# Gate pairs of a decoder layer on one Trainium2 core: the norm's product one step later, the GELU gates one pair later, and three LRU steps from GpSimd to ScalarE and VectorE

## The chip, the core and the metric

The kernel runs on one core of a Trainium2 chip: one launch computes a whole decoder layer in float32. The time is that of the device in microseconds, lower is better; the median of three runs is the figure to forecast. Five engines work side by side: TensorE does matrix products, VectorE (DVE in the profile) elementwise work and scans, ScalarE (ACT) functions and copies, GpSimd (POOL) elementwise work and the issue of transfers, SyncE (SP) the issue of transfers alone. Each runs its own instructions strictly in order, and waits for another engine or a transfer by semaphores.

## The reference, cut to what matters

```python
h = h + W_out( sum_k sigmoid(g_k(xn)) * P_k(mixer_k(xn)) )      # xn = RMSNorm(h), 1024 tokens x 1024
h = h + W2 relu(W1 RMSNorm(h))^2
# mixer A (gMLP), mixer B (RG-LRU, 8 heads of 128), mixer C (SSD, 4 groups)

# B: the LRU
r = sigmoid(xh @ w_r + b_r);  i = sigmoid(xh @ w_i + b_i)
log_a = -8 * r * softplus(-lam);  a = exp(log_a)
inp = sqrt(-expm1(2 * log_a)) * (i * xb)
h_t = a_t * h_{t-1} + inp_t
y_b = gelu(gate) * h

# C: what follows the scan of SSD
y = y * silu(z)
y_c = norm_g * y * rsqrt(mean(y * y over its group of 256 channels) + EPS)
```

All gates (`g_k`, `gate`, `z`) are column blocks of one input product `xn @ w_in`.

## The kernel before

Every product is done in three passes on halves that are split into a high and a low part (`split`, L132 on ScalarE and L133 on VectorE: high·high, high·low, low·high). Channels lie on the 128 partitions, tokens along a row, so that one output block is 128 channels by 1024 tokens; half 0 and half 1 are its first and last 512 tokens.

**Order of the stages.** The first 130 us or so form the norm and its transposes. Until about 600 us "units" follow: `one_unit` multiplies 128 columns of `w_in` by `xn` (48 matmuls, L555), hands the result to a `post` function, and calls `step`, which advances every waiting generator by one piece. These generators are the stages of the SSD groups (`ssd_stages`, four groups) and of the LRU heads (`stages` inside `lru_units`, eight heads). This part is ordered by the framework's planner, which may exchange instructions of one engine. From about 640 to 1022 us the pair loop runs, in which the order is that of the code (`manual_schedule`). Then come the products of the three branches, `w_out`, and the MLP to the end.

**An LRU head**, for each half: three matmuls (L789) for each of the two gates, tanh (L792), exp and tanh (L796, L797), two combined steps on VectorE (L798, L799), `m + 1` on GpSimd (L800), a square root on ScalarE (L801), a combined step on VectorE (L802), a product on GpSimd (L803), and the scan on VectorE (L804). Heads 6 and 7 also multiply by their GELU gate on GpSimd (L807). The GpSimd queue also issues transfers, among them the reads of `acs_d` (L657) that the next SSD group needs and the write of its output (L732).

**A pair** is 256 columns of `w_in` by 1024 tokens. A scheme with seven products instead of eight block products computes it; each product is 12 matmuls of 128x512. Kinds of pair: "t" (a branch's gate: tanh, written to scratch), "z" (SSD's output times silu(z), the norm over the group, written to `yd["c"]`) and "g" (an LRU gate). In each turn of the loop the products are p1, p2, then p4 of the pair before, then p5, p6, p3, p7, and a `step` follows each: seven steps in a turn. The operands of the next pair are made in the same turn (`cast1`, `sums1`, `sums2`, `cast12`, `cast22`, `cast34`: L132 and L133, L502 to L507).

**The norm of a z pair** is the generator `post_z(half)`, one for each half. Half 1 starts at the last step of its own turn; half 0 is done by p4 in the next turn, and idles for three steps first. Its pieces, one a step: tanh and a combined step (L949, L950); the product with SSD's output and the square (L952, L953); the sum of two squares (L955); nothing; the matmul with `ones` that sums over the channels into `vs`, and a square root (L959, L961); the reciprocal (L963); two small steps that read `vs` (L965, L966); two more (L968, L969); the scaled result and its write (L973, L974). Before, half 1's product so stands behind p5 of the turn after the z pair, and half 0's behind p4 and ahead of p5 of the turn after that.

The list `pairs` gives the order of the pairs: before, t z t g t t z t g t t z t g t z t t t.

Of the kernel before, what the change touches and what calls it, by code (L numbers as in the profile page):

```python
# [11 lines left out]
AF = mybir.ActivationFunctionType  # L12
ALU = mybir.AluOpType
# [23 lines left out]
def trunk_kernel(ctx: ExitStack, tc: tile.TileContext, x, norm_mix_g, w_in, b_gate, gmlp_ln_g, gmlp_ln_b,  # L37
# [4 lines left out]
    nc = tc.nc  # L42
    x, w_in, b_gate, out = x[0], w_in[0], b_gate[0], out[0]
# [24 lines left out]
    def nm(s):  # L68
        uid[0] += 1
        return f"{s}_{uid[0]}"  # L70

    def act(shape=(P, T), dt=F32):
        return pools[0].tile(list(shape), dt, tag="act", name=nm("a"))

    def half_(shape=(P, HF), dt=F32):
        return halfp.tile(list(shape), dt, tag="half", name=nm("h"))

    def aux():
        return auxp.tile([P, HF], F32, tag="aux", name=nm("aux"))
# [6 lines left out]
    tt = nc.vector.tensor_tensor  # L86
    stt = nc.vector.scalar_tensor_tensor
    ts = nc.vector.tensor_scalar
    actv = nc.scalar.activation
    mm = nc.tensor.matmul  # L90

    def hsl(h):
        return slice(h * HF, h * HF + HF)
# [34 lines left out]
    def split(dst_hi, dst_lo, src, eng=None, cast=None):  # L128
        if cast:
            cast.tensor_copy(out=dst_hi, in_=src)  # L130
        else:
            actv(dst_hi, src, AF.Copy)  # L132
        (eng or nc.vector).tensor_tensor(out=dst_lo, in0=src, in1=dst_hi.bitcast(F32), op=ALU.subtract)  # L133
# [99 lines left out]
    def gelu2(dst, ps, w):  # L233
        sq = act()[:, :w]
        actv(sq, ps, AF.Square)
        stt(out=sq, in0=sq, scalar=1.0 / GELU_C, in1=ps, op0=ALU.add, op1=ALU.mult)
        actv(sq, sq, AF.Tanh, scale=GELU_S * GELU_C)
        stt(out=dst, in0=sq, scalar=1.0, in1=ps, op0=ALU.add, op1=ALU.mult)  # L238
# [212 lines left out]
    for q in range(2):  # L451
# [3 lines left out]
        for i in range(4):  # L455
            g = q * 4 + i
# [79 lines left out]
    def later(gen):  # L536
        pending.append(gen)
# [33 lines left out]
    def unit_in(col, post):  # L571
        unit(w_in[:, col:col + P], X, post)


    def conv(dst, ps, taps, bias):
        actv(dst, ps, AF.Identity, scale=taps[3], bias=bias)
        for j in (1, 2, 3):
            stt(out=dst[:, j:], in0=ps[:, :T - j], scalar=taps[3 - j], in1=dst[:, j:], op0=ALU.mult, op1=ALU.add)
# [173 lines left out]
    def lru_units(h):  # L752
        S = {}

        def post_x(ps):
            xb = S["xb"] = act()
            conv(xb, ps, [va[:, LCW + j * 8 + h:LCW + j * 8 + h + 1] for j in range(4)], va[:, LCB + h:LCB + h + 1])
            wraw = lrup.tile([P, 256], F32, tag="lr", name=nm("lr"))
            tc.keep_in_program_order(nc.sync.dma_start(out=wraw[:, :P], in_=lru_w_r[0, h]))
            tc.keep_in_program_order(nc.sync.dma_start(out=wraw[:, P:], in_=lru_w_i[0, h]))  # L760
            S["w"] = [lrup.tile([P, 256], F32R, tag=f"lw{i}", name=nm("lw")) for i in range(2)]
            split(S["w"][0], S["w"][1], wraw)
            S["xs"] = []
            for half in range(2):
                p_ = half_(dt=F32R), half_(dt=F32R)
                split(p_[0], p_[1], xb[:, hsl(half)])
                S["xs"].append(p_)
            if h < PLAIN:
                later(stages(False))
            elif h == 7:  # L770
                v_group(0)

        def post_g(ps):
            S["g2"] = act()
            gelu2(S["g2"], ps, T)
            later(stages(True))

        def stages(gated):
            if not gated:
                yield  # L780
            xb, w = S["xb"], S["w"]
            y = act()
            for half in range(2):
                tk = hsl(half)
                tri_ = []
                for q in range(2):
                    ps = aux()
                    for n, (wi, ai) in enumerate(((0, 0), (0, 1), (1, 0))):
                        mm(ps, w[wi][:, q * P:(q + 1) * P], S["xs"][half][ai], start=(n == 0), stop=(n == 2))  # L789
                    t = half_()  # L790
                    o = (LBR, LBI)[q] + h
                    actv(t, ps, AF.Tanh, scale=0.5, bias=vh[:, o:o + 1])  # L792
                    tri_.append(t)
                tr, ti = tri_
                m = half_()
                actv(m, tr, AF.Exp, scale=s2[:, h:h + 1], bias=s2[:, h:h + 1])  # L796
                actv(tr, tr, AF.Tanh, scale=s1[:, h:h + 1], bias=s1[:, h:h + 1])  # L797
                stt(out=m, in0=m, scalar=1.0, in1=tr, op0=ALU.add, op1=ALU.mult)  # L798
                stt(out=tr, in0=m, scalar=2.0, in1=m, op0=ALU.add, op1=ALU.mult)  # L799
                nc.gpsimd.tensor_scalar(out=m, in0=m, scalar1=1.0, scalar2=1.0, op0=ALU.mult, op1=ALU.add)  # L800
                actv(tr, tr, AF.Sqrt, scale=-1.0 / 16)  # L801
                stt(out=ti, in0=ti, scalar=1.0, in1=xb[:, tk], op0=ALU.add, op1=ALU.mult)  # L802
                nc.gpsimd.tensor_tensor(out=ti, in0=ti, in1=tr, op=ALU.mult)  # L803
                nc.vector.tensor_tensor_scan(out=y[:, tk], data0=m, data1=ti, initial=(0.0 if half == 0 else y[:, HF - 1:HF]),  # L804
                                             op0=ALU.mult, op1=ALU.add)
            if gated:
                nc.gpsimd.tensor_tensor(out=S["g2"], in0=y, in1=S["g2"], op=ALU.mult)  # L807
                nc.gpsimd.dma_start(out=yd["b"][h], in_=S["g2"])
            else:
                nc.gpsimd.dma_start(out=hr_d[h], in_=y)  # L810

        unit_in(C_XB + h * P, post_x)
        if h >= PLAIN:
            unit_in(C_GATE + h * P, post_g)
# [4 lines left out]
    def v_group(g):  # L819
        if g < 8:  # L820
            v_of[g] = act((P, NCH, P))
            nc.gpsimd.dma_start(out=v_of[g], in_=vn_d[:, g * P:(g + 1) * P].rearrange("(c p) d -> p c d", p=P))
# [75 lines left out]
    def actx():  # L898
        return actx_pool[0].tile(list(two), F32, tag="actx", name=nm("x"))

    class Pair:
# [42 lines left out]
        def post_z(self, half):  # L944
            o, y, t = self.o[half], self.y[half], actx()
            if half == 0:
                for _ in range(3):
                    yield
            actv(t, o, AF.Tanh, scale=0.5)  # L949
            stt(out=o, in0=t, scalar=1.0, in1=o, op0=ALU.add, op1=ALU.mult)  # L950
            yield
            tt(out=o, in0=o, in1=y, op=ALU.mult)  # L952
            actv(t, o, AF.Square)  # L953
            yield
            tt(out=t[:, 0], in0=t[:, 0], in1=t[:, 1], op=ALU.add)  # L955
            yield
            yield
            vs = aux()
            mm(vs, ones, t[:, 0], start=True, stop=True)  # L959
            r, q = y[:, 0], y[:, 1]  # L960
            actv(r, vs, AF.Sqrt, scale=1.0 / 256, bias=eps4)  # L961
            yield
            nc.vector.reciprocal(out=r, in_=r)  # L963
            yield
            tt(out=q, in0=r, in1=r, op=ALU.mult)  # L965
            stt(out=q, in0=vs, scalar=256 * 4.0 * EPS, in1=q, op0=ALU.add, op1=ALU.mult)  # L966
            yield
            ts(out=q, in0=q, scalar1=-0.5 / 256, scalar2=1.5, op0=ALU.mult, op1=ALU.add)  # L968
            tt(out=r, in0=r, in1=q, op=ALU.mult)  # L969
            yield  # L970
            for b in range(2):
                col = SNG + self.e + b
                stt(out=o[:, b], in0=o[:, b], scalar=va[:, col:col + 1], in1=r, op0=ALU.mult, op1=ALU.mult)  # L973
            nc.gpsimd.dma_start(out=self.part(yd["c"], half), in_=o)  # L974
# [41 lines left out]
    pairs = [(br, e) for br in (2, 1, 0) for e in range(0, KD, 2)]  # L1016
    pairs = [("t",) + p_ for p_ in pairs]
    for i in range(3):
        pairs.insert(5 * i + 1, ("z", 0, 2 * i))
        pairs.insert(5 * i + 3, ("g", 0, 2 * i))  # L1020
    pairs.insert(15, ("z", 0, 6))
    cur = []

# [609 lines left out]
    with tc.manual_schedule():  # L1633
# [159 lines left out]
        for n in range(NB):  # L1793
            j, i = divmod(n, 7)
# [58 lines left out]
```

## Time and profile before

| | |
|---|---|
| median of 3 runs | 2010.82 us (2010.63 to 2010.97) |
| profiled execution | 2009.9 us; its span 2007.9 us |
| TensorE busy | 1923.5 us, 96% |
| VectorE, ScalarE, GpSimd busy | 1406.7 (70%), 1005.3 (50%), 293.1 us (15%) |
| mean granted clock of TensorE | 0.982 of full speed |
| stage of the pairs | about 640 to 1022 us |
| stage of SSD and LRU units | about 130 to 600 us |

How to read it: TensorE is the engine that is nearly always busy, so time can be lost in two ways only: it stands idle, or its clock is lowered. In rows of the timeline the bracket at the end of a row gives the idle time before it and what ended that; in rows of the chain the first number is the start, the second the length. Rows of the windows give, for a stretch, the busy time and instruction count of TensorE's matmuls, its weight loads, VectorE, ScalarE and GpSimd, then the granted clock, the busy share of the transfer engines and GB/s.

### The profile page before, as it was taken

How to read it: one execution, taken by the hardware profiler on the slowest of the kernel's cores; microseconds unless marked ns; L12 is line 12 of the kernel's file. 1: busy time of each engine (PE TensorE's matmuls, PEld its weight loads, DVE VectorE, ACT ScalarE, POOL GpSimd, SP SyncE). 2: the span in 40 equal slices, each digit the busy share in tenths (PEclk: the TensorE clock that was granted, in tenths of full speed). 3: DMA queues.
4: the chain of work that ended last, by engine and by line, in shares of the span. 5: the costliest groups of instructions: out<-in, count | busy, mean ns of one | idle time of the engine just before them, and what ended most of it. 6: DMA issues, size and time to landing. Idle time of an engine off the chain costs nothing.

```text
span 2007.9 us, 23777 instructions
## 1 busy us (share of the span) xinstructions
PE 1923.5 (96%) x8928; PEld 1596.5 (80%) x8928; DVE 1406.7 (70%) x2000; ACT 1005.3 (50%) x1455; POOL 293.1 (15%) x392
## 2 busy tenths in 40 slices
PE   8999999999999999998999999998999999999996
PEld 7998878787787787787788888786788887888885
DVE  5485868686668766666758789436765557787787
ACT  6425858576533445444554544246555555253243
POOL 4112313233333000000010111000111110000000
PEclk9999999999999999999999999999999999999998
DMA  4246465465654242525289787521544448644532
GB/s 158 66 140 145 118 138 132 110 146 130 146 145 139 92 147 74 171 77 162 74 277 282 208 270 193 173 95 53 168 163 137 162 155 301 193 138 135 189 109 91
DMA packets 211015, 301.25 MB, mean 150 GB/s; under 512 B 13028, under 2 KB 125876, under 8 KB 210900
## 3 DMA queue, kind: packets, MB, share of 16 engines
q1 hardware_dynamic: 167348, 158.54, 26.2%
q0 software_dynamic: 34544, 119.69, 21.9%
q10 hardware_dynamic: 9008, 21.51, 3.0%
q8 instruction: 70, 1.15, 0.2%
q14 instruction: 45, 0.37, 0.1%
HBM read 195.75 MB, written 74.58 MB: 135 GB/s over the span
## 4 chain that ended last, share of the span: by engine, by line
PE 55%; DVE 11%; ACT 6%; issue 4%; DMA 2%; POOL 0%; ACTq 0%; SPq 0%; DVEq 0%; POOLq 0%
PE aux L478 39%; PE gps L478 8%; PE ps L555 4%; PE aux L1375 2%; DMA wt<-in_w_branch_c_dram 1%; ACT wt L132 1%; DVE wt L133 1%; DMA a<-acs_d 1%; DVE a L133 1%; ACT a L1424 1%; DVE rsq_q L111 1%; PE aux L959 1%; DVE b L133 1%; ACT a L132 1%; PE aux L836 0%
## 5 line engine op out<-in xcount | busy, mean ns | idle before, releaser
L555 PE MATMUL ps<-xn,wh 128*128 128x512 f32 x1088 | 295.6, 393 | 0.0
L478 PE MATMUL aux<-b,b 128*128 128x512 f32 x1152 | 264.3, 389 | 0.3 <-DVE b L133 0.2
L478 PEld LDWEIGHTS aux<-b,b 128*128 128x128 f32 x1152 | 215.9, 188 | 46.3 <-DVE b L133 1.6
L555 PEld LDWEIGHTS ps<-xn,wh 128*128 128x128 f32 x1088 | 203.7, 189 | 42.4 <-issue 0.3
L478 PE MATMUL aux<-a,b 128*128 128x512 f32 x960 | 219.4, 389 | 0.0
L478 PEld LDWEIGHTS aux<-a,b 128*128 128x128 f32 x960 | 180.2, 188 | 37.4
L555 PE MATMUL ps<-xn,wl 128*128 128x512 f32 x544 | 167.6, 389 | 0.0
L478 PE MATMUL gps<-xn,wt 128*128 128x512 f32 x684 | 160.2, 392 | 2.1 <-DVE a L238 2.1
L478 PE MATMUL aux<-b,wt 128*128 128x512 f32 x672 | 156.9, 389 | 0.0
L478 PEld LDWEIGHTS gps<-xn,wt 128*128 128x128 f32 x684 | 129.4, 189 | 29.4 <-issue 2.5
L478 PEld LDWEIGHTS aux<-b,wt 128*128 128x128 f32 x672 | 126.2, 188 | 26.2
L133 DVE TENSOR_TENSOR wt<-a,wt 128x1024 fp32r<-128x1024 f32 x66 | 80.9, 1225 | 89.0 <-ACT wt L132 88.9
L132 ACT ACTIVATE b<-wt 128x1024 fp32r<-128x1024 f32 x88 | 90.7, 1053 | 87.3 <-DMA wt<-u_d 62.5
L555 PEld LDWEIGHTS ps<-xn,wl 128*128 128x128 f32 x544 | 102.2, 188 | 21.6
L133 DVE TENSOR_TENSOR b<-wt,b 128x1024 fp32r<-128x1024 f32 x88 | 107.2, 1219 | 17.3 <-ACT b L132 17.2
L1605 DVE TENSOR_TENSOR a<-aux,a 128x512 f32<-128x512 f32 x112 | 77.0, 688 | 50.0 <-PE aux L478 50.0
L133 DVE TENSOR_TENSOR a<-a,a 128x1024 fp32r<-128x1024 f32 (+1 forms) x68 | 66.6, 985 | 41.5 <-ACT a L132 41.5
L133 DVE TENSOR_TENSOR wt<-rt,wt 128x1024 fp32r<-128x1024 f32 x35 | 42.8, 1224 | 66.8 <-ACT wt L132 66.8
L478 PE MATMUL aux<-a,wt 128*128 128x512 f32 x336 | 78.7, 390 | 3.3 <-ACT a L1482 3.3
L132 ACT ACTIVATE a<-a 128x1024 fp32r<-128x1024 f32 (+1 forms) x68 | 55.8, 837 | 50.3 <-DVE a L1557 45.4
L478 PEld LDWEIGHTS aux<-a,wt 128*128 128x128 f32 x336 | 62.9, 188 | 17.2 <-ACT a L1482 4.2
L132 ACT ACTIVATE wt<-a 128x1024 fp32r<-128x1024 f32 x66 | 69.6, 1054 | 7.0 <-DVE a L506 6.7
(350 smaller groups left out, 3570.5 us busy)
## 6 DMA issues: line engine op xcount, KB each, us to landing
wt<-u_d SPq DMA_DIRECT2D x54, 512.0 KB
u_d<-a POOLq DMA_DIRECT2D x48, 512.0 KB, 5.6
raw<-in_w_in_dram SPq DMA_DIRECT2D x34, 512.0 KB
wl<-raw POOLq DMA_DIRECT2D x34, 512.0 KB, 5.2
g_d<-a POOLq DMA_DIRECT2D x24, 512.0 KB, 3.4
a<-g_d ACTq DMA_DIRECT2D x24, 512.0 KB
rt<-in_w_in_dram SPq DMA_DIRECT2D x19, 512.0 KB
a<-in_w_in_dram SPq DMA_DIRECT2D x19, 512.0 KB
```

What stands on the lines that cost most here:

```text
L111: stt(out=q, in0=r, scalar=nh, in1=r, op0=ALU.mult, op1=ALU.mult)
L132: actv(dst_hi, src, AF.Copy)
L133: (eng or nc.vector).tensor_tensor(out=dst_lo, in0=src, in1=dst_hi.bitcast(F32), op=ALU.subtract)
L478: mm(ps, lhs[l][kk], rhs[r][kk], start=(new and n == 0), stop=(n == 11), skip_group_check=not new)
L555: mm(ps[:, hsl(h)], w[wi][:, k, :], a.rhs(ai, k, h), start=(n == 0), stop=(n == 3 * KD - 1))
L959: mm(vs, ones, t[:, 0], start=True, stop=True)
L1375: mm(ps, M.tok(a, k, c), wo[nb][k][w], start=(k == 0 and a + w == 0), stop=(k == KD - 1 and a == 1))
L1424: actv(Nf[th, k // 2][:, k % 2, (c % 4) * P:(c % 4 + 1) * P], ps[:, i * P:(i + 1) * P], AF.Identity, scale=g2c[:, KD + k:KD + k + 1])
L1605: tt(out=h, in0=ps, in1=h, op=ALU.add)
```

## The change

Three edits:

1. `post_z` gets one more empty step between the sum L955 and the norm's matmul. The matmul, and every later piece of the generator with it, stands one step (one product) later.
2. Each of the three "g" pairs stands one place later in the list. The order becomes t z t t g t z t t g t z t t g z t t t.
3. In the LRU stages `m + 1` becomes a ScalarE activation, and the products L803 and, for the two gated heads, L807 become VectorE tensor-tensor instructions.

```diff
@@ LRU stages
-                nc.gpsimd.tensor_scalar(out=m, in0=m, scalar1=1.0, scalar2=1.0, op0=ALU.mult, op1=ALU.add)
+                actv(m, m, AF.Identity, bias=1.0)
                 actv(tr, tr, AF.Sqrt, scale=-1.0 / 16)
                 stt(out=ti, in0=ti, scalar=1.0, in1=xb[:, tk], op0=ALU.add, op1=ALU.mult)
-                nc.gpsimd.tensor_tensor(out=ti, in0=ti, in1=tr, op=ALU.mult)
+                tt(out=ti, in0=ti, in1=tr, op=ALU.mult)
...
             if gated:
-                nc.gpsimd.tensor_tensor(out=S["g2"], in0=y, in1=S["g2"], op=ALU.mult)
+                tt(out=S["g2"], in0=y, in1=S["g2"], op=ALU.mult)
@@ post_z
             tt(out=t[:, 0], in0=t[:, 0], in1=t[:, 1], op=ALU.add)
             yield
             yield
+            yield
             vs = aux()
@@ pairs
         pairs.insert(5 * i + 1, ("z", 0, 2 * i))
-        pairs.insert(5 * i + 3, ("g", 0, 2 * i))
+        pairs.insert(5 * i + 4, ("g", 0, 2 * i))
```

From L955 on, line numbers after the change are one higher (L959 becomes L960). Where the instructions now stand, at three places:

TensorE, two turns after the first z pair, before. `gps_5718` is what p4 adds to, `aux_5917` is p5's result, `ones` the norm's operand of half 0:

```order
L478 MATMUL gps_5718<-a_5433,a_5693 128x512
L478 MATMUL gps_5718<-a_5432,a_5693 128x512
L959 MATMUL aux_5914<-x_5771,ones 128x512
L478 MATMUL aux_5917<-h_5061,wt_5810 128x512
L478 MATMUL aux_5917<-h_5062,wt_5810 128x512
```

The same place after the change, where `aux_5914` is p5's result and `gps_5857` is what p6 adds to:

```order
L478 MATMUL gps_5718<-a_5432,a_5693 128x512
L478 MATMUL aux_5914<-h_5061,wt_5807 128x512
...
L478 MATMUL aux_5914<-h_5401,wt_5808 128x512
L960 MATMUL aux_5934<-x_5771,ones 128x512
L478 MATMUL gps_5857<-h_4972,wt_5807 128x512
```

All 12 matmuls of p5 now stand between p4 and the norm's matmul of half 0, which is the first row ahead of p6.

VectorE, the rows that lead to half 0's sum (L955), before. `x_5655` belongs to half 1, `a_5602` and `x_5771` to half 0; `wt_5875` is an operand of the next turn:

```order
L963 RECIPROCAL x_5655<-x_5655 128x512
L1001 TENSOR_TENSOR a_5785<-aux_5772,a_5785 128x512
L133 TENSOR_TENSOR a_5828<-a_5715,a_5828 128x512
L965 TENSOR_TENSOR x_5655<-x_5655 128x512
L966 SCALAR_TENSOR_TENSOR x_5655<-aux_5792,x_5655 128x512
L950 SCALAR_TENSOR_TENSOR a_5602<-x_5771,a_5602 128x1024
...
L952 TENSOR_TENSOR a_5602<-a_5602,x_5709 128x1024
L133 TENSOR_TENSOR wt_5875<-a_5789,wt_5874 128x1024
L973 SCALAR_TENSOR_TENSOR a_5653<-a_5653,va,x_5655 128x512 x2
L955 TENSOR_TENSOR x_5771<-x_5771 128x512
```

And after, the names as before but for the operand, which is `wt_5873`:

```order
L1002 TENSOR_TENSOR a_5785<-aux_5772,a_5785 128x512
L133 TENSOR_TENSOR a_5827<-a_5715,a_5827 128x512
L964 RECIPROCAL x_5655<-x_5655 128x512
L950 SCALAR_TENSOR_TENSOR a_5602<-x_5771,a_5602 128x1024
...
L952 TENSOR_TENSOR a_5602<-a_5602,x_5709 128x1024
L133 TENSOR_TENSOR wt_5873<-a_5789,wt_5872 128x1024
L969 TENSOR_SCALAR x_5655<-x_5655 128x512
L970 TENSOR_TENSOR x_5655<-x_5655 128x512
L955 TENSOR_TENSOR x_5771<-x_5771 128x512
L986 TENSOR_TENSOR a_5870<-gps_5879,a_5870 128x512
L974 SCALAR_TENSOR_TENSOR a_5653<-a_5653,va,x_5655 128x512 x2
```

Half 1's reciprocal moved behind two rows of the pair, half 1's L969 and L970 moved to just ahead of half 0's sum, and the two scaling rows (before L973, now L974) moved from ahead of that sum to behind it.

GpSimd, where the last SSD group begins beside LRU head 6, before. `h_` tiles and `a_4335` are the LRU's, `a_4528` and `a_4531` the rows of `acs_d` that the SSD group needs, `a_4490` is the gMLP's input:

```order
L800 TENSOR_SCALAR h_4380<-h_4380 128x512
L800 TENSOR_SCALAR h_4402<-h_4402 128x512
L803 TENSOR_TENSOR h_4378<-h_4378,h_4372 128x512
L803 TENSOR_TENSOR h_4400<-h_4400,h_4394 128x512
L822 DMA a_4490<-vn_d 128x8x128
L807 TENSOR_TENSOR a_4335<-a_4367,a_4335 128x1024
L657 DMA a_4528<-acs_d 128x512
L808 DMA yb_d<-a_4335 128x1024
```

And after:

```order
L528 DMA wl_4417<-raw_4414 128x1024
L822 DMA a_4490<-vn_d 128x8x128
L657 DMA a_4528<-acs_d 128x512 x2
L657 DMA a_4531<-acs_d 128x512
L808 DMA yb_d<-a_4335 128x1024
```

The five computing rows are gone from the queue, and three reads of `acs_d` stand ahead of the write of the LRU's output. In three SSD groups the planner also changed ScalarE's order around the first step of a convolution (L576), which before stood behind a split of the LRU's weights (L132 `lw`) that waits for a transfer:

```order
L527 ACTIVATE wl_4040<-wh_4039 128x1024
L632 ACTIVATE a_4015<-a_4010 128x1024
L132 ACTIVATE lw_4208<-lr_4205 128x256
L526 ACTIVATE wh_4146<-raw_4144 128x1024
L576 ACTIVATE a_4093<-ps_4044,vh,scw 128x1024
```

and after stands ahead of it:

```order
L527 ACTIVATE wl_4040<-wh_4039 128x1024
L632 ACTIVATE a_4015<-a_4010 128x1024
L576 ACTIVATE a_4093<-ps_4044,vh,scw 128x1024
L526 ACTIVATE wh_4146<-raw_4144 128x1024
L132 ACTIVATE lw_4208<-lr_4205 128x256
```

The split with its wait moved behind the convolution's first step. ScalarE has 45 loads of a function table before and after.

## The prediction

> **What bounds the kernel now.** I read the page first, then TensorE's table of waits, then its timeline at the longest of them, the chain of waits there, and the clock by windows.
>
> ```profile
> span 2007.9 us, 23777 instructions
> PE 1923.5 (96%) x8928; PEld 1596.5 (80%) x8928; DVE 1406.7 (70%) x2000; ACT 1005.3 (50%) x1455; POOL 293.1 (15%) x392
> ```
>
> TensorE is the bound: it rests 84 of 2007.9 us. The change takes no matmul away, so it can gain only idle time and lowered clock. Who makes TensorE wait (total, times, longest):
>
> ```profile
> PE aux L959 <- DVE x L955: 19.3, 4, 4.8
> PE aux L789 <- ACT a L677: 4.2, 1, 4.2
> PE aux L789 <- DVE h L714: 3.3, 2, 2.0
> PE aux L478 <- ACT a L991: 3.0, 3, 1.0
> PE aux L703 <- DVE h L673: 2.1, 2, 1.2
> PE aux L703 <- ACT a L576: 2.1, 1, 2.1
> PE aux L789 <- DVE h L729: 1.9, 3, 0.6
> ```
>
> The first row is the norm's matmul, four waits for four z pairs. The timeline of TensorE shows it undisturbed for half 1 (674.55), and with its wait for half 0 (696.71); the last two rows frame the same place of the fourth z pair:
>
> ```profile
> 671.82 2.89 PE L478 MATMUL aux<-h,wt 128*128 128x512 f32 x12
> 674.55 1.02 PE L959 MATMUL aux<-x,ones 128*128 128x512 f32 x2
> 678.14 2.88 PE L478 MATMUL aux<-xn,wt 128*128 128x512 f32 x12
> ...
> 689.02 2.88 PE L478 MATMUL gps<-a,a 128*128 128x512 f32 x12
> 696.71 2.04 PE L959 MATMUL aux<-x,ones 128*128 128x512 f32 x2 [4.81 <-DVE x L955]
> 697.77 5.37 PE L478 MATMUL aux<-h,wt 128*128 128x512 f32 x12
> 702.98 2.90 PE L478 MATMUL gps<-h,wt 128*128 128x512 f32 x12
> ...
> 987.62 2.88 PE L478 MATMUL gps<-a,a 128*128 128x512 f32 x12
> 1000.64 2.88 PE L478 MATMUL gps<-h,wt 128*128 128x512 f32 x12
> ```
>
> One product takes 674.55 − 671.82 = 2.73 us, a turn of seven 19.1. Two products and the norm take 678.14 − 671.82 = 6.32 us undisturbed, 702.98 − 689.02 = 13.96 with the wait: it costs 7.64, of which 4.8 is idle and 2.8 slow clock (p5 at 697.77 took 5.37 instead of 2.88). For the fourth it is 13.02 − 6.32 = 6.70. Three times 7.64 and 6.70 are 29.6 us. When a wait costs clock is read from the granted clock (the number after the five busy columns):
>
> ```profile
> 476.00:478.00 2.00, 1.52 (x5) 1.22 (x6) 2.00 (x11) 0.93 (x3) 0.00 (x0) 0.71 0.84 202
> 478.00:480.00 2.00, 2.00 (x6) 1.61 (x5) 1.16 (x2) 1.20 (x2) 0.00 (x0) 0.50 0.16 46
> ...
> 290.00:300.00 10.00, 8.71 (x39) 1.00 0.69 160
> ```
>
> The first two rows follow the 2.0 us wait of the L714 row: 2 × (0.29 + 0.50) = 1.6 us of clock lost. The last, of TensorE alone, holds the other of that row's two waits, 3.3 − 2.0 = 1.3 us, and keeps the full clock. So here 1.3 us is free of a clock penalty, 2.0 is not. The Trainium skill, page "TensorE: Matmul & The Clock Gate", section "What's actually happening", puts the halving behind at least one idle window of about 3.4 us, free-running; this trace shows it after 2.0, so the row decides.
>
> **The norm one product later.** What makes half 0 late is read from the chain there:
>
> ```profile
> 681.14 3.26 DVE x L963
> ...
> 688.60 0.35 DVE x L968
> ...
> 688.97 0.69 DVE x L969
> 689.66 1.15 DVE a L952
> ...
> 690.89 1.06 ACT x L953
> ...
> 694.56 0.42 DVE a L973
> ...
> 695.22 0.75 DVE a L973
> 695.97 0.61 DVE x L955
> ```
>
> TensorE ended p4 at 689.02 + 2.73 = 691.7. With p5 (2.73) put ahead of the norm it has work to 694.4. L955 must then be done by 694.4 but was done at 696.6: without any other movement 2.2 us of wait would be left. The new order on VectorE moves it too: half 1's two L973 rows (694.56 to 695.97, 1.4 us) no longer stand ahead of L955; instead half 1's L968 and L969 do (0.35 + 0.69 = 1.04). These two stood ahead of L952 and now stand behind it, so L952 can come 1.04 earlier; I take 0.8, since the 3.3 us of L963 now start behind two rows of the pair that wait for p3. So L955 is done at 696.6 − 0.8 − (1.4 − 1.04) = 695.4, and the matmul comes 0.1 to 0.3 later (696.58 to 696.71 before): a wait of 1.3 us remains, by the row above without clock loss. Its two ends are 0 and 2.2 with clock loss; I take 1.3 by the walk. The gain is 29.6 − 4 × 1.3 = 24.4 us. Half 1's matmul stands behind p6, with its sum long done (at 674.55 it already had no wait): nothing. The norm's result is needed for the write to scratch alone, which no pair reads; nothing else queues behind it on TensorE but p6.
>
> **The gate pairs one place later.** This costs no instruction. It removes a collision: half 0's L973 came in the turn of the "g" pair, in front of that pair's own GELU steps. The row L478 <- L991 (3.0 in three waits, 1.0 each) is the turn behind each "g" pair. There ScalarE's L991 stands behind the GELU's tanh, which waits for VectorE's chain that began with those two L973 rows (1.4 us) and behind a table load, an unhidden 1.28 us by the table-load row further down. Both are gone from that place in the new order, 2.7 us against a wait of 1.0: +2.3 us taken (ends 0 and 3.0). The fetch of rows for the "g" pair sits on SP's queue:
>
> ```profile
> SPq L925 <- DVE a L973: 59.8, 3, 19.9
> ```
>
> It waits there 20 us each time for a z pair's buffers, with the next weights queued behind it; the later place gives a turn (19 us) more, the later L974 takes back 2.7. No row shows TensorE waiting for those weights, so I cost it at nothing; were the cover gone, they would come later by 2.7 us at most.
>
> **What is given back at the merge.** The first branch product after the pairs needs the last z pair's output from scratch. Rows of SP, GpSimd and TensorE:
>
> ```profile
> 1003.26 13.46 SPq L1104 DMA_DIRECT2D a<-yc_d  x2
> 1016.77 6.47 SPq L1093 DMA_DIRECT2D wt<-in_w_branch_c_dram  x4
> ...
> 1012.32 0.71 POOL L974 DMA_DIRECT2D yc_d<-a  x1
> ...
> 1053.11 9.27 PE L478 MATMUL aux<-b,b 128*128 128x512 f32 x38 [0.23 <-DVE b L133]
> ```
>
> SP's read of `yc_d` holds back the branch weights until the write of 1012.32 has landed, and TensorE meets the end of that string at 1053.11 with only 0.23 us of wait: no slack. TensorE comes there earlier by the 5.4 us that the last z pair saves, while L974 is one step (2.7 us) later than before in its turn. The string starts about when it did, so between 2.7 and 5.4 us come back; I take 4.
>
> **LRU.** Rows of the groups, 130 to 530 us:
>
> ```profile
> L803 POOL TENSOR_TENSOR h<-h,h 128x512 f32<-128x512 f32 x16 | 21.3, 1334 | 6.7 <-ACT h L801 6.7
> L801 ACT ACT_TABLE_LOAD x14 | 18.0, 1283 | 0.2
> L800 POOL TENSOR_SCALAR h<-h 128x512 f32<-128x512 f32 x16 | 11.6, 723 | 69.0 <-DVE h L799 69.0
> L801 ACT ACTIVATE h<-h 128x512 f32<-128x512 f32 x16 | 10.0, 633 | 1.3 <-DVE h L799 1.1
> L807 POOL TENSOR_TENSOR a<-a,a 128x1024 f32<-128x1024 f32 x2 | 4.8, 2392 | 4.2 <-DVE a L804 4.2
> ```
>
> GpSimd loses 21.3 + 11.6 + 4.8 = 37.7 us. ScalarE gains 16 × 0.63 = 10.1, VectorE 16 × 0.69 and 2 × 1.15 (the lengths of L969 and L952 in the chain above) = 13.3. The cover:
>
> ```profile
> 450.00:526.00 76.00, 68.85 (x336) 56.31 (x336) 49.58 (x75) 49.80 (x82) 24.46 (x32) 0.96 0.57 129
> ```
>
> VectorE and ScalarE rest 26 of 76 us there, and their added 23 us are spread over 300. Within a head the path grows: before, L801 (0.63) and L803 (1.33) led to the scan; now 0.63, a table load of 1.28 behind it, 0.63 and 0.69. Nothing but the scan and its write waits for that, while later ScalarE rows are pushed by 0.63. Of the seven waits above five lie in this stage, 4.2 + 3.3 + 2.1 + 2.1 + 1.9 = 13.6, and with a clock loss of 1.6 behind the three of 2.0 or more, 18.4 us are the most to be had. The worst end is 16 × 0.63 = 10.1 us lost, each added ScalarE row on TensorE's path. The 4.2 wait follows an `acs_d` read that stood behind L807 (2.39) and two L803 (some 1.3 of their 2.67 replaced by VectorE rows): about 3.6 earlier, so it and its clock loss give 5.2. The waits of 2.0 and 2.1 hang on a convolution step (L576) that stood behind L132 `lw`; it now comes 1 to 5 us earlier (L526's 1.0, and a wait of 4.6 on average for the weights' transfer). That removes both with their clock, 7.3, if it reaches TensorE whole; I take half. Together 5.2 + 3.7 = 9 us.
>
> **Sum.** 24.4 + 2.3 − 4 + 9 = 31.7 us. From the profiled execution's 2009.9 (span 2007.9) that makes 1978.2; the median of the runs is 0.9 higher, 1979.
>
> **Rivals.**
> A, the LRU part brings nothing. The small waits on ScalarE and VectorE grow as fast as those on GpSimd's reads go. For it: the five rows name VectorE and ScalarE, which get the work. Against: the 4.2 wait is behind GpSimd's queue. 2010.8 − 22.7 = 1988, and 1996 with 8 of the worst 10 us lost.
> B, L955 isn't earlier. ScalarE's L953 and the casts end where they did: 2.2 us of wait, and the clock falls as after 2.0 (1.6): 3.8 each instead of 1.3. 10 us less, 1989. For it: VectorE is filled between 680 and 696. Against: the order shows the two scaling rows behind L955. By the Trainium skill's rule of the same page and section, a gap of 2.2 us would leave the clock alone, and B would end 6.4 us lower, near 1983; the 478 us window speaks against that.
> C, the other side: ScalarE becomes the bound in the LRU heads. `m + 1` now stands ahead of each table load, so each half carries 0.63 + 1.28 = 1.91 us that a wait for VectorE's L799 used to cover; 16 of them are 30.6 against the 22.7 saved elsewhere: 2019. It decides from 12 of the 16 on TensorE's path. Against: ScalarE rests a third of the stage, and a unit's matmuls need its results only one unit later.
> D, all goes well: every LRU wait gone (18.4) and nothing given back: 1979 − 9.4 − 4 = 1966.
> That the edits do nothing is excluded by the order of the rows: the matmul does stand behind p5.
>
> **How the numbers follow.** Forecast 0.60 (its own range 1969 to 1990, from the ends of the norm's wait and the LRU term), A 0.17, B 0.12, D 0.07, C 0.04. The range 1966 to 1996 leaves out C, half of D and the tail of A, some 0.15. Within 0.2% (4 us, about what a measurement of this kernel can tell from no change) would need A's worst end and B at once: 0.02. Slower comes from C, 0.03; faster 0.95.
>
> **What would show it.** Right: the row L960 <- L956 has four waits of about 1.3 us or none, the windows behind them keep the full clock, and p5 takes 2.9 us again; L478 <- L992 falls below 1 us in total; the wait at the first sums of the merge grows from 0.2 to about 4; the L677 wait falls below 1 us. Wrong: clock at 0.50 behind the norm (B), or new waits of TensorE on L792, L796 or L800 between 200 and 530 us (A, C).

## The result, and the profile after

The changed kernel takes 1976.12 us in the median of four runs (1975.50 to 1979.05); the kernel before took 2010.72 (four runs, 2009.44 to 2010.97). The ratio is 0.9832, 95% interval 0.9815 to 0.9849. The forecast was 1979 us, range 1966 to 1996. The profiled execution, 1979.05 us, is the longest of the four; its page:

```profile
span 1977.3 us, 23724 instructions
PE 1914.5 (97%) x8928; PEld 1592.9 (81%) x8928; DVE 1409.4 (71%) x2018; ACT 1015.5 (51%) x1471; POOL 256.9 (13%) x358
```

TensorE's waits (total, times, longest):

```profile
PE aux L703 <- DVE h L673: 4.4, 2, 3.1
PE aux L960 <- DVE x L955: 3.1, 4, 0.8
PE aux L703 <- ACT a L576: 3.0, 1, 3.0
PE aux L789 <- DVE h L714: 1.3, 1, 1.3
PE aux L478 <- ACT a L992: 0.5, 3, 0.2
```

The norm's four waits went from 19.3 to 3.1 us, those behind the "g" pairs from 3.0 to 0.5. The waits on L677 and L729 are gone; one of the two on L714 is left. But L576 and L673, in the LRU and SSD stage, rose from 2.1 each to 3.0 and 4.4. TensorE's timeline at the first z pair, and the windows there (five busy columns, then the clock):

```profile
687.26 2.88 PE L478 MATMUL aux<-h,wt 128*128 128x512 f32 x12
690.92 1.10 PE L960 MATMUL aux<-x,ones 128*128 128x512 f32 x2 [0.78 <-DVE x L955]
691.45 3.30 PE L478 MATMUL gps<-h,wt 128*128 128x512 f32 x12
```

```profile
690.00:692.00 2.00, 1.22 (x4) 0.63 (x4) 2.00 (x5) 1.18 (x2) 0.00 (x0) 1.00 0.77 188
692.00:694.00 2.00, 2.00 (x11) 1.64 (x10) 2.00 (x4) 1.97 (x3) 1.00 (x2) 1.00 1.07 358
```

p5 (687.26) runs ahead of the norm in 2.88 us, the wait is 0.78, and the clock stays full. The chain of waits there shows the walk that the prediction made, with L969 and L970 where the two scaling rows stood:

```profile
684.13 1.14 DVE a L952
...
685.36 1.06 ACT x L953
...
687.88 1.23 DVE wt L133
689.11 0.35 DVE x L969
...
689.48 0.69 DVE x L970
690.17 0.61 DVE x L955
```

Where the time went, stage by stage. The stages are parted by the start of the first matmul of the units, of their last one on the high half of the weight (`wh`, L555), of the first merge product and of the first `w_out` product (L1375, now L1376):

| stage | before | after | gained |
|---|---|---|---|
| up to the units | 126.1 | 128.8 | −2.7 |
| units (SSD, LRU, gMLP) | 490.9 | 483.8 | 7.1 |
| end of units, pairs | 410.8 | 382.9 | 27.9 |
| merge | 232.5 | 234.8 | −2.3 |
| rest | 747.6 | 747.0 | 0.6 |
| span | 2007.9 | 1977.3 | 30.6 |

The first row holds code that the change does not touch; its 2.7 us are about what the profiled execution is longer than the median (2.9). The merge gives back what the prediction's string of `yc_d` rows said, in three small waits where there had been one of 0.23:

```profile
997.57 0.97 PE L478 MATMUL aux<-a,a 128*128 128x512 f32 x3 [1.31 <-DVE a L133]
...
1033.56 2.01 PE L478 MATMUL aux<-b,b 128*128 128x512 f32 x6 [0.33 <-DVE b L133]
1036.10 24.09 PE L478 MATMUL aux<-b,b 128*128 128x512 f32 x105 [0.53 <-DVE b L133]
```

### The profile page after: what moved, and what is told of

The parts are those of the page before. It is cut to its first block, busy times and chain, and to the rows that moved or that the text cites. A ratio compares the mean times of both kernels' runs of the same rounds, so it can differ in the third digit from the quotient of the medians.

```text
span 1977.3 us, 23724 instructions
## 1 busy us (share of the span) xinstructions
PE 1914.5 (97%) x8928; PEld 1592.9 (81%) x8928; DVE 1409.4 (71%) x2018; ACT 1015.5 (51%) x1471; POOL 256.9 (13%) x358
## 4 chain that ended last, share of the span: by engine, by line
PE 68%; DVE 11%; issue 7%; ACT 7%; DMA 6%; POOL 1%; ACTq 0%; POOLq 0%; DVEq 0%; SPq 0%
PE aux L478 39%; PE ps L555 10%; PE gps L478 8%; PE aux L257 5%; PE aux L1376 2%; DMA a<-acs_d 2%; DVE a L578 1%; DMA raw<-in_w_in_dram 1%; DMA c<-yc_d 1%; ACT a L1425 1%; DMA wl<-raw 1%; PE aux L789 1%; DVE a L133 1%; DVE rsq_q L111 1%; DVE wt L133 1%
## 5 line engine op out<-in xcount | busy, mean ns | idle before, releaser
L555 PE MATMUL ps<-xn,wh 128*128 128x512 f32 x1088 | 294.8, 392 | 0.0
L555 PEld LDWEIGHTS ps<-xn,wh 128*128 128x128 f32 x1088 | 202.9, 188 | 42.1 <-issue 0.7
L555 PE MATMUL ps<-xn,wl 128*128 128x512 f32 x544 | 167.6, 389 | 0.0
L132 ACT ACTIVATE b<-wt 128x1024 fp32r<-128x1024 f32 x88 | 90.9, 1054 | 85.5 <-DMA wt<-u_d 55.3
L555 PEld LDWEIGHTS ps<-xn,wl 128*128 128x128 f32 x544 | 102.1, 188 | 21.5
L132 ACT ACTIVATE a<-a 128x1024 fp32r<-128x1024 f32 (+1 forms) x68 | 55.9, 838 | 53.4 <-DVE a L1558 45.1
L132 ACT ACTIVATE wt<-a 128x1024 fp32r<-128x1024 f32 x66 | 69.6, 1054 | 8.8 <-DVE a L506 8.3
```

The costliest lines, as they stand in the source:

```text
L555: mm(ps[:, hsl(h)], w[wi][:, k, :], a.rhs(ai, k, h), start=(n == 0), stop=(n == 3 * KD - 1))
```

## The experiments

Ratios are to runs of the kernel before on the same chip. They come with the experiment, since these runs spread more than the first four (2006.6 to 2014.7). Medians of different experiments can come from different chips; their ratios compare better.

**Each edit by itself.** Edit 1 (one more `yield`), edit 2 (`5 * i + 4`), both, and edit 3 (the three LRU steps):

> Edit 1 alone: the norm's product one step later, the "g" pairs and the LRU as before. Theory (the norm's wait is most of the gain, and it does not need the other edits): the four waits of the norm's matmul fall from 19.3 us to about 3, with full clock behind them; 29.6 - 3.1 = 26.5 us gained, the waits of 1.0 us behind the "g" pairs stay: about 1985 us. Rival (the later L974 collides with the GELU of the "g" pair, which is why those were moved): each wait behind a "g" pair grows by a step, 2.7 us, 8 us in all: about 1993 us.

> Edit 2 alone: the "g" pairs one place later, the norm and the LRU as before. Theory: only the waits on L991 go, 3.0 to about 0.5 us: 2008 us, and the norm still waits 19 us in all. Rival (the "g" pair's work on VectorE is what makes half 0's sum late): the norm's waits fall as well, about 1990 us.

> Edits 1 and 2, the LRU as before. Theory: the stage of the pairs gives 27.9 us and the merge takes 2.3 back: about 1985 us, so that the LRU edit is worth 7 to 9 of the whole. Rival (the LRU edit is worth nothing): about 1976 us, the time of the whole change.

> Edit 3 alone. Theory: the stage of the units becomes 7 us shorter, the rest as before: about 2003 us. Rival (nothing gained, the waits only change their place): about 2010 us. Second rival (ScalarE on the path): above 2012 us.

| edits | median us | ratio | 95% interval |
|---|---|---|---|
| 1 | 2005.1 | 0.9973 | 0.9963 to 0.9982 |
| 2 | 2006.8 | 0.9984 | 0.9971 to 0.9997 |
| 1 and 2 | 1981.3 | 0.9863 | 0.9848 to 0.9877 |
| 3 | 1999.8 | 0.9955 | 0.9940 to 0.9970 |

Edit 2 came out as its theory said: the waits on L991 fell from 3.0 to 0.5 us and the norm still waited 19.2. Edits 1 and 2 came out 4 us below their theory, so that edit 3 is worth 5 to 6 us beside them; edit 3 alone came out 3 us below its own. Edit 1 was expected at 1985 and came out at 2005: the theory failed, and its rival (1993) was too mild. The norm's waits did fall, from 19.3 to 3.1 us. What replaced them is in the waits and the timeline of edit 1 alone:

```profile
PE aux L478 <- ACT a L992: 14.3, 3, 4.8
...
PE aux L960 <- ACT a L992: 2.3, 3, 0.8
```

```profile
697.03 1.10 PE L960 MATMUL aux<-x,ones 128*128 128x512 f32 x2 [0.78 <-ACT a L992]
...
724.68 4.38 PE L478 MATMUL aux<-xn,wt 128*128 128x512 f32 x12 [4.76 <-ACT a L992]
```

The wait moved one turn on, behind each "g" pair, with the same 4.8 us and again a loss of clock (12 matmuls in 4.38 us, where 2.88 is usual; behind the two later ones they took 5.01 and 5.37). Edit 2 alone gains 3 us. Together they gain 29, not 5 + 3: edit 2 is worth 24 us once edit 1 is there. The chain of edit 1 alone, from the reciprocal of half 0 to that wait:

```profile
704.11 3.26 DVE x L964
...
710.47 1.06 ACT x L935
...
711.55 1.28 ACT L937
...
714.39 0.96 ACT wt L132
...
716.51 1.41 DVE a L974 x2
717.92 1.13 DVE a L939
...
719.57 1.22 DVE a L941
720.79 1.14 DVE wt L133
721.92 1.15 DVE x L936
...
724.05 0.59 ACT a L992
```

TensorE is not in it: VectorE and ScalarE hand the work to and fro, with the norm's reciprocal (3.26) and scaling (1.41) in the same string as the GELU. Counted from the start of the p5 that follows the z pair (673.46 here, 671.82 before), TensorE ends p6, ahead of the wait, 46.3 us later instead of 52.9, so 6.6 sooner. L992 starts 50.6 us later, where L991 before started 53.5 later: only 2.9 sooner. The difference of 3.7 is the growth of the wait from 1.0 to 4.76. The old wait at the norm had given this string the time it needs.

**Is it VectorE's backlog?** Edit 1 alone, the reciprocal only for half 1:

```diff
-            nc.vector.reciprocal(out=r, in_=r)
+            if half:
+                nc.vector.reciprocal(out=r, in_=r)
```

> Edit 1 alone, and the reciprocal of half 0 (3.35 us on VectorE) left out in the four z pairs, so that the norm of these halves is not computed rightly. In the run of edit 1 alone the wait had moved behind the "g" pairs (three of 4.8 us). Theory (VectorE has too much to do in the turn that holds half 0's norm and the "g" pair's GELU, and the 4.8 us are its backlog): the wait behind each "g" pair falls by 3 us or more, to about 1.5 and without clock loss: about 1990 us. Rival (the late rows of the "g" pair on SP's queue, or ScalarE's table load of 1.28 us, set it): the waits stay at 4 to 4.8 us, about 2004 us.

1987.6 us, ratio 0.9885 (0.9870 to 0.9900). The timeline behind the first "g" pair:

```profile
722.73 3.01 PE L478 MATMUL aux<-xn,wt 128*128 128x512 f32 x12 [1.58 <-ACT a L993]
```

Taking 3.3 us of VectorE out of that turn took 3.2 us off the wait, and the loss of clock with it: 17 us for four reciprocals. The backlog theory holds; the table load and SyncE's queue, both unchanged, do not set the 4.8 us by themselves.

**One step more still.** The whole change with one more `yield`:

> The whole change with one more empty step, so that the norm's matmul stands two products later than at first. Theory: its four waits of 0.78 us go (3.1 us), the later write of the last z pair gives 2 to 3 us back at the merge: 1974 to 1976 us. Rival (half 0's norm again reaches into the turn of the "g" pair, as with edit 1 alone): waits of 2 us or more behind the "g" pairs, above 1982 us.

1983.3 us, ratio 0.9862 (0.9847 to 0.9877): 7 us slower than the change. The norm waits no more, but TensorE has four new waits, one in each z pair, and a long one at the merge:

```profile
701.10 3.02 PE L478 MATMUL gps<-a,a 128*128 128x512 f32 x12 [1.11 <-DVE a L1007]
...
997.41 1.03 PE L478 MATMUL aux<-a,a 128*128 128x512 f32 x2 [4.96 <-ACT a L132]
```

Now the reciprocal stands ahead of the pair's own L1007 on VectorE, for which p4 waits, and the last z pair's output is written too late for the merge. Both expectations missed: the direction of the rival was right, its place was not.

**The z pairs closer together.** The whole change, with the pairs as t z t t g z t t g z t t g z t t t t t:

```diff
-        pairs.insert(5 * i + 1, ("z", 0, 2 * i))
-        pairs.insert(5 * i + 4, ("g", 0, 2 * i))
-    pairs.insert(15, ("z", 0, 6))
+        pairs.insert(4 * i + 1, ("z", 0, 2 * i))
+        pairs.insert(4 * i + 4, ("g", 0, 2 * i))
+    pairs.insert(13, ("z", 0, 6))
```

> The whole change with the z and g pairs in groups of four places instead of five (t z t t g z t t g z t t g z t t t t t), so that the last z pair is done two turns, 38 us, sooner. Theory: the write of its output no longer holds the branch weights at the merge, whose waits (1.31, 0.33 and 0.53 us) go: about 1974 us. Rival (a z pair directly behind a g pair collides with its GELU on VectorE): new waits of 1 to 5 us with loss of clock, 1980 us or more.

1972.2 us, ratio 0.9805 (0.9789 to 0.9822). In its timeline the only wait between the last z pair and `w_out` is one of 0.20 us:

```profile
1029.64 30.71 PE L478 MATMUL aux<-b,b 128*128 128x512 f32 x134 [0.20 <-DVE b L133]
```

So the merge's waits did come from the last z pair's late write. The rival is out: behind the "g" pairs the waits stay at 0.5 us in all, as in the whole change. The 4 us by medians lie at the edge of what the two intervals tell apart.

**Which part of the LRU edit.** The whole change, but `m + 1` on GpSimd as before:

> Edits 1 and 2, and of edit 3 only the products L803 and L807 on VectorE; m + 1 stays on GpSimd. Theory (the gain of edit 3 comes from GpSimd's queue, which the products held for longer): the time of the whole change within 2 us, about 1976 to 1978. Rival (m + 1 on ScalarE is worth most, since with it the planner puts the convolution's step L576 ahead of the wait for the LRU's weights): 1981 us, that of edits 1 and 2. Second rival (m + 1 on ScalarE costs): 1973 us.

1975.6 us, ratio 0.9822 (0.9808 to 0.9837): the time of the whole change. `m + 1` on ScalarE is worth nothing that this run shows; with it undone the planner also puts L576 behind the wait for the LRU's weights again, and the wait on L576 is 2.0 us, shorter than the 3.0 with the new order. With the pairs closer together the same undoing gave:

> The kernel with the pairs in groups of four, m + 1 again on GpSimd. Theory (m + 1 on ScalarE is worth nothing, as the run with the pairs in groups of five showed): 1972 us within 2. Rival (it was worth something that the other run's spread hid): 1975 us or more.

1975.4 us, ratio 0.9830 (0.9815 to 0.9844) against 0.9805: the intervals overlap, and the profiles show five waits of TensorE in the units each, 7.9 us with `m + 1` on GpSimd and 8.2 without; the units take 482.6 and 483.7 us. Whether `m + 1` is worth 0 or 3 us stays open.

**What is left in the units.** The chain of the changed kernel ahead of its 3.1 us wait on L673:

```profile
445.18 0.04 POOLq L528
445.22 2.55 issue
...
447.79 0.85 POOL wl L528
448.64 0.57 POOL yr_d L732
449.21 0.76 POOL a L657 x2
449.97 9.83 DMA a<-acs_d
```

The reads of `acs_d` stand on GpSimd's queue behind L528, the second half of a weight, which waits for its transfer and for ScalarE. They stood there before the change too, and then behind L732, which waited for VectorE:

```profile
444.11 0.85 POOL L528 DMA_DIRECT2D wl<-raw  x1 [10.57 <-ACT wl L527]
446.93 0.57 POOL L732 DMA_DIRECT2D yr_d<-h  x1 [1.97 <-DVE h L731]
447.49 2.16 POOL L657 DMA_DIRECT2D a<-acs_d  x4
```

Counted from the start of the units (126.1 before, 128.8 after), the reads now go out 1.3 us sooner (447.49, 448.89), but the last that this chain needs lands no sooner (456.81, 459.80). TensorE, on the same count, comes to its wait on L673 1.7 us sooner (467.16, 468.21). So most of the growth of that wait, from 0.9 to 3.1 us, is TensorE's earlier arrival. Two kernels with the pairs closer together issue them elsewhere:

```diff
-                    nc.gpsimd.dma_start(out=e[:, cc], in_=acs_v[0, ...
+                    nc.scalar.dma_start(out=e[:, cc], in_=acs_v[0, ...     # or nc.sync.dma_start
```

> The kernel with the z and g pairs in groups of four (1972 us), and the reads of acs_d (L657) issued from ScalarE's queue instead of GpSimd's. What is left of TensorE's waits in the LRU stage is 7 to 9 us and hangs on these reads. Theory (they stand on GpSimd's in-order queue behind L528, which waits for a weight transfer): the reads start some 3 us or more sooner, the waits of 2.9 and 2.6 us on L576 and L673 go with their clock loss: 1965 to 1967 us. Rival (the transfer engines are full, and a read that starts sooner lands no sooner): 1972 us. Second rival (ScalarE's queue is held up by the issue): above 1974 us.

> As the kernel before, but the reads of acs_d on SyncE's queue, where they stand between the weight transfers (L523), each of which waits for a buffer. Theory (what delays the reads is a queue that waits for weights): no gain, since SyncE's queue waits for the same weights: 1971 to 1974 us. Rival (GpSimd's own issue is slow): as on ScalarE's queue, below 1968 us.

ScalarE: 1976.9 us, 0.9839 (0.9824 to 0.9853), slower than on GpSimd; a new wait of 4.86 us at 201 us. In the chain of that wait the first group's reads go out at 178.40, right behind ScalarE's L632, which had waited for VectorE's L578, so this queue has a waiting row ahead of them as well. SyncE: 1961.5 us, 0.9761 (0.9742 to 0.9781), the fastest of all, where no gain was expected. No wait of TensorE is left between 130 and 600 us, and the units take 469.1 us instead of 483.7. The rows of the issues, first on SyncE's queue, then the same reads on GpSimd's in the kernel with the pairs closer together:

```profile
431.94 0.38 SPq L523 DMA_DIRECT2D raw<-in_w_in_dram  x1
432.42 2.66 SPq L657 DMA_DIRECT2D a<-acs_d  x4
```

```profile
444.97 0.85 POOL L528 DMA_DIRECT2D wl<-raw  x1 [10.54 <-ACT wl L527]
445.51 0.88 POOL L732 DMA_DIRECT2D yr_d<-h  x1
446.07 2.49 POOL L657 DMA_DIRECT2D a<-acs_d  x4
```

The four issues take as long on SyncE's queue (2.66 us) as on GpSimd's (2.49), so the rival, a slow issue on GpSimd, is out, although the time lies in its range. Both queues wait for weights, but SyncE's entry stands right behind the issue of one (431.94), not behind its landing. The idea (a read stuck behind a weight) was right; the expectation for SyncE was wrong because I looked at what its queue waits for and not at which side of the wait the reads stand on.

**The LRU edit without its queue.** That fastest kernel with edit 3 undone:

> The fastest kernel so far (pairs in groups of four, reads of acs_d on SyncE's queue: 1961.5 us), with edit 3 undone: m + 1 and the products of the LRU on GpSimd again. Theory (edit 3 gains 9 us because its products stood ahead of the reads of acs_d in GpSimd's queue; with the reads on another queue there is nothing left to gain): 1961 to 1964 us, and no wait on L677. Rival (the products cost on their own, through VectorE's scans that wait for them or through the later results of the LRU): 1968 us or more, with waits of 0.6 us on L729 back.

1982.8 us, ratio 0.9859 (0.9842 to 0.9875), 21 us slower: the theory failed. The waits and one row of SyncE's timeline:

```profile
PE aux L703 <- ACT a L576: 7.8, 2, 4.8
...
PE aux L703 <- DVE h L673: 5.0, 1, 5.0
...
PE aux L789 <- DVE h L729: 1.9, 3, 0.6
```

```profile
359.87 0.38 SPq L523 DMA_DIRECT2D raw<-in_w_in_dram  x1
360.29 2.74 SPq L657 DMA_DIRECT2D a<-acs_d  x4
```

With other costs in the LRU the planner put these reads behind the next weight on SyncE's queue; the same reads of the same group went out at 344.50 in the fastest kernel. Counted from the start of the units, the reads of the three groups that TensorE waits for went out 10, 16 and 25 us later than in the fastest kernel. These waits are 12.8 us and their loss of clock 8.5, so nearly all of the 21 us is again the place of the reads, and the run cannot say what the products cost by themselves. No wait on L677 came back, as the theory said. The three waits of 0.6 on L729, which the rival named, did come back: 1.9 us of idle time that the products on GpSimd do cost. An order fixed by hand for these reads would tell the rest apart; it wasn't tried.

## Why the prediction was right, and where not

- **The norm's product** (24.4 us with its remaining wait). Right in mechanism and size in the whole change: the walk gave waits of 1.3 us without loss of clock, they were 0.78 with full clock; the stage of the pairs gained 27.9 us against 24.4 + 2.3. Rival B (L955 not earlier) is out. That a wait of 2.0 us costs clock, by which B and the 2.2 us end were priced, holds in some executions only (last section).
- **The gate pairs** (+2.3 us, ends 0 and 3.0). This step failed in its size. Alone it gains 3 us, about as said, but beside edit 1 it decides 24. I took the 1.0 us behind the "g" pairs as all that their turn could cost. It was so small only because TensorE had just waited 4.8 us at the norm, in the same turn, while VectorE caught up. The prediction asked what is late next for L955, not for the turn's last row once TensorE comes 5 us sooner. The sum came out because both edits were made together; as a split between the two it is luck.
- **SyncE's wait for the "g" pair's rows** (nothing). It holds so far as the profiles show: no wait of TensorE on those weights appears with the pairs in either place.
- **The merge** (4 us back). 2.3 in the profiles, a little under the lower end (2.7) of its range; the kernel with the last z pair earlier shows the cause.
- **LRU** (9 us). 7.1 in the profiles, 10.6 by the medians of edit 3 alone, 5 to 6 beside edits 1 and 2. In five profiles without edit 3 the units took 488.5 to 491.5 us, in four with it and the reads on GpSimd 481.4 to 483.8. The 4.2 us wait behind L807 went, as said. The step on L576 failed in part. In the last group, counted from the start of the units, L576 came 4.4 us sooner (441.68 before, 440.00 after), but the reads of `acs_d` that follow from it only 1.3, since L528 then held them. The wait on L576 itself grew from 2.1 to 3.0, although what it waits for came 0.8 us sooner, and that on L673 from 0.9 to 3.1: at both places TensorE came 1.7 us sooner. The 2.0 on L714, put down to the same step, fell to 0.4, which the profile puts down to L237. The three waits on L729 (1.9) fell away, which was not foreseen. So the term was right in sum and in part by luck. Rivals A and C (ScalarE) are out: added ScalarE rows cost nothing that the run with `m + 1` on GpSimd shows.

## What to carry to other kernels

A wait of the bounding engine is also time in which the others catch up: before counting it as gained, walk the helpers' rows of the next stretch with the bounding engine's arrival moved earlier by it, and look whether their string fits. Two generators with long chains on the same helper belong in different turns. For a read in an in-order queue, look which waiting row it stands behind, ahead of asking which engine issues it: issuing these reads elsewhere gained 11 us by the medians (9 by the ratios), and 21 were lost in the run in which they stood behind one more weight of that queue.

## What the runs showed of the hardware

TensorE's clock behind a wait. In the stages of the units and the pairs of all 14 profiles, every listed wait up to 1.84 us kept the full clock, and every one of 3.41 us or more lost some of it. Between 1.85 and 3.14 us it went both ways: 27 of 41 waits lost clock, 14 did not, and the length does not say which. The same 8 matmuls behind a wait of the same length at the same place, first with the whole change, then with edit 3 only:

```profile
471.32 3.18 PE L703 MATMUL aux<-h,a 128*128 128x256 f32 x8 [3.11 <-DVE h L673]
```

```profile
467.92 2.23 PE L703 MATMUL aux<-h,a 128*128 128x256 f32 x8 [3.14 <-DVE h L673]
```

3.18 us against 2.23, where the granted clock stayed at 1.00. With the reads on ScalarE's queue a wait of 1.85 us was enough: 3.07 us for these matmuls. A loss is not in proportion to the wait either: behind the norm's four equal waits of 4.8 us before the change, the granted clock stood at 0.50 for 6.8 us three times and for 3.4 us once. The Trainium skill, page "TensorE: Matmul & The Clock Gate", section "What's actually happening", describes a free-running window of about 3.4 us; that it runs freely fits waits of one length that end both ways, but its length as the least idle time does not fit a loss after 1.85 us.
